# Seven block products for eight in the pooled gate of a two-layer decoder trunk

## The chip, the core and the metric

The kernel runs on one core of a Trainium2 chip. TensorE (PE; its weight loads are listed as PEld) multiplies 128x128 blocks and writes PSUM. VectorE (DVE), ScalarE (ACT) and GpSimd (POOL) work in SBUF. SP issues most of the transfers, and each engine takes its instructions in the order in which they stand in its queue. The metric is the device time of one execution in microseconds, as the median of several runs.

## The reference

Two decoder layers work on 528 tokens (16 learned meta tokens in front of 512), model width 1024, in float32. Each layer makes one projection of the normalised stream, runs two token mixers on its parts, and adds the gated sum of both back:

```
h = rmsnorm(h_res, norm_gain[l])
proj = h @ w_in[l]
u_pool, z_pool, c_q, c_kv, k_rope, z_mla, g_pool, g_mla = jnp.split(proj, IN_SPLIT_POINTS, axis=-1)
y_pool = (pool_mix(u_pool, ...) * jax.nn.silu(z_pool)) @ pool_w_up[l]
o_mla = mla(c_q, c_kv, k_rope, ...)
y_mla = (o_mla * jax.nn.silu(z_mla)) @ mla_w_up[l]
merged = jax.nn.sigmoid(g_pool) * y_pool + jax.nn.sigmoid(g_mla) * y_mla
h_res = h_res + merged @ w_out[l]
```

`pool_mix` takes causal means over windows of 2, 4, 8 and 16 tokens. `mla` is causal attention with 8 heads, a normalisation of queries and keys and a rotary part. The "pooled gate" of the title is `g_pool`, 1024 outputs of the 1024 inputs, thus eight tiles of 128 outputs with eight input blocks of 128 each. The output leaves the meta tokens out. The inputs' gains are scaled by 8, the meta tokens by 3.559.

## The kernel before, in words

**Precision.** Every large product is made from three passes. A float32 operand is split into a rounded high part and a residual: ACT copies the high part in fp32r, DVE subtracts it (`split`, L275, and for weights `wload`, L170 to L182). `mm3` (L184) then multiplies high by high, high weight by low input, and low weight by high input into one PSUM bank.

**The stream of weights.** `register` (L909) appends every matrix product of a layer to `plan` as a `Gemm`, in the order ckv, cq0 to cq4, u with k, v, zp with y, cq5, qr and qn (queries), pu (pooled output), zm, gp (the pooled gate), gm (the other gate), mu and o. `stream` (L193) walks through the plan as a generator in chunks of 512 weight columns, which are four input blocks of a tile. For each chunk it takes the oldest of four prepared ones, issues the load, ACT split and DVE residual of a later chunk, and issues the matmuls. It yields after every second block what these should take, columns over 2.4 GHz, so that the rest of the code can count planned time. Weight chunks arrive in three `raw` buffers on SP's queue; three `whi`/`wlo` pairs hold the split ones.

**Layer input.** x times the norm's gain is split into the eight pairs `hh`/`hl` (`split_h`, L332), without the reciprocal norm of the token. That one, `self.inv` (tile `rinv`), is known later, so it is multiplied in at eviction: L496 for u, L505 for zp and zm, L573 for the pooled gate, L873 for the other one.

**Segments.** Layer 0 computes all 528 tokens, in two halves of 264 columns, each in its own PSUM bank. Layer 1 (`last`) needs only the 512 true tokens for most products, in one segment of 512. Tiles named `mm` share four PSUM banks; the attention's transposes (L796) and its output pieces (L824) take theirs from the same four. Scores have three banks (`S`) and the head's output has one (`o`).

**Attention as host for the gates.** `go` (L973) drives a layer. After the queries come their norm statistics (`qk_stats`, L665) and the preparation of head 0; then eight heads follow. Each head has its scores, a masked row minimum on DVE (L730), exponentials on ACT (L737), row sums, a multiplication on POOL (L774, L776), and transposes and output products one head later (`pv`, L779). Four times per head `gap` (L970) lets the stream run for `FILL[l]` of planned time, so pu, zm, gp and most of gm are worked off between the pieces of the heads. `fill_now` does the same at fixed places. What is issued is then put in order by a scheduler at build time, so the pieces interleave on each engine.

**The gate's eviction.** For each tile m and segment `ev_gp` (L570) multiplies PSUM by `rinv` on DVE (L573), takes tanh on ACT (L574), and DVE forms (tanh + 1) times the pooled output in place (L575; `self.am[m]` is `xb[:, m]`, which held x before). The residual `wlo` of each weight chunk is L181, its high part L180.

Of the kernel before, what the change touches and what calls it, by code (L numbers as in the profile page):

```python
# [9 lines left out]
F32 = mybir.dt.float32  # L10
# [8 lines left out]
P = 128  # L19
# [33 lines left out]
FILL = (2950.0, 2850.0)  # L53
# [18 lines left out]
def trunk(ctx, tc, xT, pos, win, wkr, wqb, wkb, wvb, wgr, wpu, wmu, wout, gains, const, yT):  # L72
# [23 lines left out]
    def sqt():  # L96
        return tp.tile([P, HALF], F32, tag="sq", name=nm("sq"), bufs=14)

# [68 lines left out]

    loads = [0]
# [15 lines left out]
    def mm3(out, wh, wl, xh, xl, start, stop):  # L184
        pe.matmul(out, wh, xh, start=start, stop=False)  # L185
        pe.matmul(out, wh, xl, start=False, stop=False)  # L186
        newest[0] = pe.matmul(out, wl, xh, start=False, stop=stop)  # L187
# [5 lines left out]
    def stream():  # L193
# [3 lines left out]
        def load(i):  # L197
            g_, c = flat[i]
            n = min(512, g_.width - c)
            return wload(g_.src[:, c:c + n], n, g_.gain, g_.spare)  # L200
# [109 lines left out]

    hbuf = [(slot(f"hh{k}", F32R), slot(f"hl{k}", F32R)) for k in range(8)]

    class Layer:
        def __init__(self, l):
            self.l, self.last = l, l == DEPTH - 1
            self.XS = XTOK if self.last else FULL
            self.x0 = NM if self.last else 0
            self.xt = xt if l == 0 else [None] * 8
# [7 lines left out]
            self.sq = []  # L326
            self.st = self.acc = self.inv = self.cinv = self.kraw = self.kp = None
# [171 lines left out]
        def ev_silu(self, dst, tag, m):  # L499
            def ev(ps, a, b):  # L500
                if a == self.x0:
                    dst[m] = slot(f"{tag}{m}") if tag == "u" else xb[:, m]
# [6 lines left out]
            return ev  # L509

# [59 lines left out]
        def ev_gp(self, m):  # L570
            def ev(ps, a, b):
                t = tmp()
                dve.tensor_mul(t[:, :b - a], ps, self.inv[:, a:b])  # L573
                act.activation(t[:, :b - a], t[:, :b - a], AF.Tanh, scale=0.5)  # L574
                dve.scalar_tensor_tensor(out=self.am[m][:, a:b], in0=t[:, :b - a], scalar=1.0,  # L575
                                         in1=self.am[m][:, a:b], op0=ALU.add, op1=ALU.mult)
            return ev
# [87 lines left out]
        def qk_stats(self):  # L665
# [20 lines left out]
            fill_now(9500)  # L686
# [28 lines left out]
        def head(self, h, kq, prev):  # L715
            kh, kl, qh, ql = kq
            odd = h % 2
            nqs = self.nqs
# [6 lines left out]
            def scores(i, out, a, b):  # L725
                q0 = NM + P * i
                mm3(out, qh[:, q0:q0 + P], ql[:, q0:q0 + P], kh[:, a:b], kl[:, a:b], True, True)
# [51 lines left out]
        def pv(self, prev, js):  # L779
# [38 lines left out]
            if odd == 1:  # L818
# [3 lines left out]
                def part2():  # L822
# [5 lines left out]
                    dve.tensor_mul(f, f, self.zms[p][:, NM:T])  # L828
# [34 lines left out]
        def meta_out(self, p):  # L863
            f = tmp()
            dve.tensor_mul(f[:, 0:NM], self.mo[:, NM * p:NM * (p + 1)], self.zms[p][:, 0:NM])
# [43 lines left out]
        def register(self, nxt):  # L909
# [24 lines left out]
            def zp(m):  # L934
                add(f"zp{m}", wi(MT_ZP + m), D, evac=self.ev_silu(self.zps, "xa", m), xs=hs, segs=XS)
# [20 lines left out]
            for m in range(4):  # L956
                add(f"zm{m}", wi(MT_ZM + m), D, evac=self.ev_silu(self.zms, "u", m), xs=hs, segs=XS)
            for m in range(8):
                add(f"gp{m}", wi(MT_GP + m), D, evac=self.ev_gp(m), xs=hs, segs=XS)
# [13 lines left out]
        def go(self, nxt):  # L973
            l = self.l
            up = lambda name: upto((l, name))
            if l == 0:
# [11 lines left out]
            up("u1")  # L988
            for m in range(2):
                self.mix(m, self.window(m))  # L990
            up("u3")
            s2 = self.window(2)
            up("k3")
            s3 = self.window(3)
            up("zp0")
            self.mix(2, s2)
            up("zp1")
            self.mix(3, s3)
            self.k_factors()
            up("qr1")  # L1000
            for s, (a, b) in enumerate(FULL):
                a0 = max(a, self.x0)
                self.stat(self.acc[:, a0:b], a0, b, C_CQ, self.acc_last)
            up("qn3")
            self.qk_stats()
            fill_now(2600)
# [103 lines left out]
```

## Time and profile before

| | |
|---|---|
| time, median of 3 runs | 790.52 us (789.74 to 790.87) |
| span of the profiled execution, first to last instruction | 787.1 us |
| median less span (start and end outside the instructions) | 3.4 us |
| matmuls recorded | 5301 |
| weight chunks split (L180, L181) | 251 and the first |
| transfers | 81.83 MB, mean 104 GB/s |
| first score matmul of head 0, layer 0 and 1 | 174.6 and 571.5 us |
| stage of the pooled gate's evictions, layer 0 and 1 | 210 to 274 and 605 to 658 us |

One execution of its own was profiled; its total is not listed apart from its span. A row of a group names line, engine, operation, tiles and shape, then the count, the total busy time, the mean of one in ns, and the idle time before it with what ended it. Matmul ends are modelled and overlap, so their pace is read from starts. Idle time of an engine that is not the bottleneck costs nothing.

### The profile page before, as it was taken

To read this page: it belongs to the slowest core of one execution; us is meant where nothing else is said; L and a number is where in the kernel's file an instruction comes from. 1 tells how busy PE (TensorE), PEld (TensorE's weight loads), DVE (VectorE), ACT (ScalarE), POOL (GpSimd) and SP (SyncE) were. 2 spreads that over 40 slices of the span, in tenths; PEclk is the share of its full clock that TensorE was granted. 3 is DMA by queue.
4 is the path that set the end of the run, shared out by engine and by line. 5 is a ranking of instruction groups with operands and counts; after the bars stand their busy time and mean duration, and the time that the engine had idled before them with its cause. 6 is when DMAs were issued, how large, how long until landed. Compare 5 with 4: busy or idle time off the path is not lost.

```text
span 787.1 us, 14567 instructions
## 1 busy us (share of the span) xinstructions
PE 780.9 (99%) x5301; PEld 708.6 (90%) x5301; DVE 535.1 (68%) x1165; ACT 410.8 (52%) x930; POOL 194.4 (25%) x259
## 2 busy tenths in 40 slices
PE   9999999999999999999999999999999999999998
PEld 8999899999999999999997898887788888887887
DVE  5848787446779987675464487775467888755932
ACT  7645655635656565633354356455445666554420
POOL 1034504002333242051000145131022333410500
PEclk9999999999999999999999999999999999999999
DMA  6242333423223212224642422334232222122372
GB/s 242 82 102 85 96 120 102 128 81 94 96 76 92 78 58 78 95 81 146 192 123 94 95 88 90 129 88 136 96 105 88 95 84 82 65 81 67 102 242 84
DMA packets 52263, 81.83 MB, mean 104 GB/s; under 512 B 8784, under 2 KB 17360, under 8 KB 52192
## 3 DMA queue, kind: packets, MB, share of 16 engines
q1 hardware_dynamic: 52048, 80.65, 32.9%
q8 instruction: 41, 0.67, 0.4%
q14 instruction: 30, 0.25, 0.1%
q10 hardware_dynamic: 144, 0.26, 0.1%
HBM read 74.49 MB, written 4.27 MB: 100 GB/s over the span
## 4 chain that ended last, share of the span: by engine, by line
PE 95%; DMA 2%; DVE 1%; issue 1%; ACT 0%; SPq 0%; ACTq 0%
PE mm L185 28%; PE mm L187 28%; PE mm L186 28%; PE mm L796 2%; PE S L186 2%; PE S L187 1%; PE S L185 1%; PE o L802 1%; PE o L801 1%; PE S L453 1%; DMA xb<-xT 1%; PE mm L355 1%; DVE wlo L181 1%; PE mm L412 0%; DMA rinv<-win 0%
## 5 line engine op out<-in xcount | busy, mean ns | idle before, releaser
L185 PE MATMUL mm<-hh,whi 128*128 128x264 f32 (+2 forms) x1096 | 346.7, 318 | 0.2 <-ACT racc L810 0.2
L186 PE MATMUL mm<-hl,whi 128*128 128x264 f32 (+2 forms) x1096 | 343.9, 315 | 0.0
L187 PE MATMUL mm<-hh,wlo 128*128 128x264 f32 (+2 forms) x1096 | 343.0, 315 | 0.0
L181 DVE TENSOR_TENSOR wlo<-raw,whi 128x512 fp32r<-128x512 f32 (+2 forms) x251 | 188.6, 755 | 119.6 <-ACT whi L180 115.9
L180 ACT ACTIVATE whi<-raw 128x512 fp32r<-128x512 f32 (+2 forms) x251 | 150.4, 601 | 187.5 <-PE mm L186 126.5
L185 PEld LDWEIGHTS mm<-hh,whi 128*128 128x128 f32 x1096 | 205.9, 188 | 13.6 <-ACT racc L810 0.5
L186 PEld LDWEIGHTS mm<-hl,whi 128*128 128x128 f32 x1096 | 206.6, 189 | 11.8
L187 PEld LDWEIGHTS mm<-hh,wlo 128*128 128x128 f32 x1096 | 205.5, 188 | 12.0
L774 POOL TENSOR_TENSOR pm<-pa,rs 128x16 f32<-128x16 f32 x32 | 11.6, 361 | 181.3 <-DVE rs L769 181.3
L560 POOL TENSOR_TENSOR racc<-racc,tmp 128x264 f32<-128x264 f32 (+1 forms) x15 | 14.2, 948 | 153.8 <-ACT tmp L559 129.8
L702 POOL TENSOR_TENSOR tmp<-kp,bc 64x528 f32<-64x528 f32 x16 | 22.5, 1408 | 76.9 <-PE mm L675 44.5
L884 POOL TENSOR_TENSOR tmp<-tmp,xb 128x264 f32<-128x264 f32 (+1 forms) x24 | 27.1, 1149 | 58.2 <-DVE tmp L882 33.1
L730 DVE CUSTOM_DVE_ANT_0 S<-S,maskw,nqs 128x272 f32<-128x272 f32 (+4 forms) x80 | 38.5, 498 | 4.2 <-PE S L187 3.9
L737 ACT ACTIVATE cq<-S,bia 128x400 f32<-128x400 f32 (+2 forms) x48 | 24.6, 516 | 22.6 <-DVE bia L764 12.0
L185 PE MATMUL mm<-u,whi 128*128 128x264 f32 (+1 forms) x108 | 35.2, 326 | 0.0
L187 PE MATMUL mm<-cq,wlo 128*128 128x264 f32 (+1 forms) x108 | 34.5, 323 | 0.7 <-DVE wlo L181 0.7
L187 PE MATMUL mm<-u,wlo 128*128 128x264 f32 (+1 forms) x108 | 34.8, 323 | 0.0
L185 PE MATMUL mm<-cq,whi 128*128 128x264 f32 (+1 forms) x108 | 34.6, 320 | 0.0
L186 PE MATMUL mm<-cq,whi 128*128 128x264 f32 (+1 forms) x108 | 34.5, 321 | 0.0
L277 DVE TENSOR_TENSOR tl<-mm,th 128x512 fp32r<-128x512 f32 (+1 forms) x64 | 29.3, 481 | 6.1 <-ACT th L276 5.1
L776 POOL TENSOR_TENSOR cq<-cq,rs 128x384 f32<-128x384 f32 (+1 forms) x32 | 32.8, 1025 | 0.0
L186 PE MATMUL mm<-kn,whi 128*128 128x264 f32 (+1 forms) x96 | 30.7, 321 | 0.0
(252 smaller groups left out, 1362.4 us busy)
## 6 DMA issues: line engine op xcount, KB each, us to landing
raw<-win SPq DMA_DIRECT2D x143, 256.0 KB, 2.6
raw<-wout SPq DMA_DIRECT2D x32, 256.0 KB, 2.7
bc<-kdr SPq DMA_DIRECT2D x16, 264.0 KB, 3.6
raw<-wpu SPq DMA_DIRECT2D x16, 256.0 KB, 2.7
raw<-wmu SPq DMA_DIRECT2D x16, 256.0 KB, 2.5
raw<-wqb SPq DMA_DIRECT2D x12, 256.0 KB, 2.6
tmp<-xT SPq DMA_DIRECT2D x16, 132.0 KB, 3.0
tmp<-scr SPq DMA_DIRECT2D x7, 256.0 KB, 3.4
```

Of the source, the lines that this page charges most:

```text
L180: act.activation(hi[:, :n], raw[:, :n], AF.Copy)
L181: dve.tensor_sub(lo[:, :n], raw[:, :n], hi[:, :n].bitcast(F32))
L185: pe.matmul(out, wh, xh, start=start, stop=False)
L186: pe.matmul(out, wh, xl, start=False, stop=False)
L187: newest[0] = pe.matmul(out, wl, xh, start=False, stop=stop)
L277: dve.tensor_sub(lo[:, a:b], src, hi[:, a:b].bitcast(F32))
L702: gp.tensor_mul(kf[r0:r0 + 64, :], self.kp[r0:r0 + 64, :], bc[r0:r0 + 64, :])
L730: dve.tensor_tensor_reduce(out=sv, in0=sv, in1=mask, scale=nqs[:, i, h:h + 1], scalar=3e38, op0=ALU.add, op1=ALU.min, accum_out=bia[:, c:c ...
L737: act.activation(pv, sv, AF.Exp, scale=-1.0, bias=bia[:, i:i + 1], accum_out=rs[:, c:c + 1])
L776: gp.tensor_mul(pt[i][:, NM:], pt[i][:, NM:], rs[:, i:i + 1].to_broadcast([P, n - NM]))
L796: pe.transpose(tr[:, P * (i - j):P * (i - j + 1)], pt[i][:, NM + P * j:NM + P * (j + 1)], ident)
L884: gp.tensor_add(t[:, :b - a], t[:, :b - a], self.am[m][:, a:b])
```

## The change

The eight gate tiles are taken in four pairs and the input in two halves of four blocks and two halves of tokens. Each pair is then a 2x2 product of blocks, and Strassen's scheme in Winograd's form makes it from seven products in place of eight. That takes sums of weight blocks and of input blocks, and additions of the products.

- *Input sums.* They need one input for both token halves, so the input must be fully normalised. `reload` fetches blocks 0 to 3 of x anew from DRAM (blocks 4 to 7 still lie in `xb`), `renorm` multiplies each of the eight by gain and `rinv` and writes `hh`/`hl` again, and `mixed` forms the four sums per block pair and splits them. This stands behind the first query tiles, in and behind the query statistics, and in head 0.
- *Weight sums.* `weight_sums` forms them in DRAM (`wsum`), from copies issued by SP and accumulating transfers issued by POOL, in ten steps from the second u tile to the third query tile. Each waits for the newest matmul.
- *Products.* `fast` registers one Gemm with 28 chunks. Product 2 accumulates on product 1's bank, and product 3 of one pair on product 5's bank, after the next pair's product 1. ACT copies product 1; the others are combined by five DVE additions or subtractions per pair.
- *Evictions.* As the input is normalised, `got_gp`, `ev_zm` and `ev_gm` leave the multiplication by `rinv` out. A factor of a half of the silu of z_mla moves into the multiplications by `zms`.
- *Constants.* `FILL` shrinks, some fixed fills around the query statistics change, and in head 0 a score product is held behind the newest matmul.

```diff
-FILL = (2950.0, 2850.0)
+FILL = (2770.0, 2700.0)
...
-    def mm3(out, wh, wl, xh, xl, start, stop):
-        pe.matmul(out, wh, xh, start=start, stop=False)
...
+    def mm3(out, wh, wl, xh, xl, start, stop, more=False, hold=False):
+        first = pe.matmul(out, wh, xh, start=start, stop=False, skip_group_check=more)
+        if hold:
+            behind(first, newest[0])
...
+        def ev_zm(self, m):
+            def ev(ps, a, b):
...
+                act.activation(t[:, :b - a], ps, AF.Tanh, scale=0.5)
+                dve.scalar_tensor_tensor(out=self.zms[m][:, a:b], in0=t[:, :b - a], scalar=1.0, in1=ps,
+                                         op0=ALU.add, op1=ALU.mult)
...
+        def reload(self, k):
+            self.f[k] = slot("kl" if k % 2 else "kh", bufs=2)
+            sp.dma_start(self.f[k][:, self.x0:T], scr[:, k, :] if self.last else xT[:, k, :])
+
+        def renorm(self, k):
...
+            f, (hh, hl) = self.f[k][:, self.x0:T], self.hs[k]
+            dve.scalar_tensor_tensor(out=f, in0=x[:, self.x0:T], scalar=self.g(G_H + k), in1=self.inv[:, self.x0:T],
+                                     op0=ALU.mult, op1=ALU.mult)
+            split(hh, hl, f, self.x0, T)
+
+        def mixed(self, k):
...
+            dve.tensor_sub(w[:, b:c], u[:, b:c], w[:, b:c])
+            dve.tensor_sub(u[:, b:c], u[:, a:b], u[:, b:c])
+            dve.tensor_sub(u[:, a:b], u[:, a:b], w[:, b:c])
+            dve.tensor_sub(w[:, a:b], w[:, a:b], u[:, a:b])
+            split(th, tl, u[:, a:c], a, c)
+            for h_, l_, v in ((t3h, t3l, w[:, b:c]), (t4h, t4l, w[:, a:b])):
+                split(h_, l_, v, 0, n)
...
+        def fast(self, name, w, got):
+            order = []
+            for u in range(4):
+                order += [(1, u)] + [(3, u - 1)] * (u > 0) + [(p, u) for p in (6, 7, 2, 5, 4)]
+            order.append((3, 3))
...
+                for k in range(4):
+                    xh, xl = (t[:, s[0]:s[1]] for t in self.hs[k + o]) if p < 4 else self.tt[k][p]
+                    c = P * k
+                    mm3(ps, w_[0][:, c:c + P], w_[1][:, c:c + P], xh, xl, k == 0 and p not in (2, 3), k == 3, True)
...
+                if p == 1:
+                    v["q", u] = q = svt()[:, :n]
+                    act.activation(q, ps, AF.Copy)
+                elif p == 2:
+                    got(2 * u, A, ps, True)
+                elif p == 6:
+                    v["u", u] = t = svt()[:, :n]
+                    dve.tensor_sub(t, v["q", u], ps)
+                elif p == 7:
+                    v["v", u] = t = svt()[:, :n]
+                    dve.tensor_sub(t, ps, v["u", u])
+                elif p == 5:
+                    t = tmp()[:, :n]
+                    dve.tensor_sub(t, v["v", u], ps)
+                    got(2 * u + 1, B, t, False)
...
+        def weight_sums(self, i, w):
...
+                if s == 0:
+                    for i, t in enumerate((b[:, 0:512], a[:, 0:512], a[:, 0:512], a[:, 512:1024])):
+                        behind(sp.dma_start(d[:, i, :], t), newest[0])
+                else:
+                    for i, t in ((0, b[:, 512:1024]), (2, b[:, 0:512])):
+                        behind(gp.dma_start(d[:, i, :], t, accum_op=ALU.add), newest[0])
+            if 0 < u < 5:
+                d = wsum[l][u - 1]
+                behind(gp.dma_start(d[:, 3 if s else 1, :], d[:, 1 if s else 0, :], accum_op=ALU.add), newest[0])
...
-                t = tmp()
-                dve.tensor_mul(t[:, :b - a], ps, self.inv[:, a:b])
-                act.activation(t[:, :b - a], t[:, :b - a], AF.Tanh, scale=0.5)
-                dve.scalar_tensor_tensor(out=self.am[m][:, a:b], in0=t[:, :b - a], scalar=1.0,
-                                         in1=self.am[m][:, a:b], op0=ALU.add, op1=ALU.mult)
...
+        def got_gp(self, m, s, v, psum):
+            am = self.am[m][:, s[0]:s[1]]
+            t = tmp()[:, :s[1] - s[0]] if psum else v
+            act.activation(t, v, AF.Tanh, scale=0.5)
+            dve.scalar_tensor_tensor(out=am, in0=t, scalar=1.0, in1=am, op0=ALU.add, op1=ALU.mult)
...
-            fill_now(9500)
+            for k in range(2):
+                self.mixed(k)
+                fill_now(2000)
+            for k in range(2, 4):
+                self.renorm(k)
+                self.renorm(k + 4)
+                fill_now(2500)
...
-                d = self.gms[m][:, a:b]
-                dve.tensor_mul(d, ps, self.inv[:, a:b])
-                act.activation(d, d, AF.Tanh, scale=0.5)
+                act.activation(self.gms[m][:, a:b], ps, AF.Tanh, scale=0.5)
...
-            for m in range(8):
-                add(f"gp{m}", wi(MT_GP + m), D, evac=self.ev_gp(m), xs=hs, segs=XS)
+            self.fast("gp", [wi(MT_GP + m) for m in range(8)], self.got_gp)
...
+            up("qn0")
+            sums()
+            for k in range(2):
+                self.renorm(k)
+                self.renorm(k + 4)
+                up(f"qn{k + 1}")
+            sums()
             up("qn3")
             self.qk_stats()
-            fill_now(2600)
             kq = self.prep(0)
             fill_now(2600)
+            self.mixed(2)
...
             for h in range(H):
                 kn_ = self.head(h, kq, prev)
                 self.gap()
+                if h == 0:
+                    self.mixed(3)
```

More of the change, by code (lines that the diff above doesn't have):

```diff
@@ L717, in head @@
             odd = h % 2
-            nqs = self.nqs
+            nqs, hold = self.nqs, h == 0
             pa = slot("pa", bufs=2, w=416)
@@ L726, in scores @@
                 q0 = NM + P * i
-                mm3(out, qh[:, q0:q0 + P], ql[:, q0:q0 + P], kh[:, a:b], kl[:, a:b], True, True)
+                mm3(out, qh[:, q0:q0 + P], ql[:, q0:q0 + P], kh[:, a:b], kl[:, a:b], True, True,
+                    hold=hold and i == 1)
             def top(i, c, sv, mask):
@@ L975, in go @@
             up = lambda name: upto((l, name))
+            made = iter(range(10))
+            sums = lambda: self.weight_sums(next(made), [win[l, MT_GP + m] for m in range(8)])
             if l == 0:
@@ L999, in go @@
             self.k_factors()
+            sums()
+            up("zp3")
+            sums()
+            up("cq5")
+            sums()
+            up("qr0")
+            sums()
+            for k in range(4):
+                self.reload(k)
             up("qr1")
```

91 lines of the change are left out of this document (79 added, 12 removed).

## The prediction

> **What bounds the kernel now.** I read the page first, its busy line, its slices and its chain of waits.
>
> ```profile
> span 787.1 us, 14567 instructions
> PE 780.9 (99%) x5301; PEld 708.6 (90%) x5301; DVE 535.1 (68%) x1165; ACT 410.8 (52%) x930; POOL 194.4 (25%) x259
> PE   9999999999999999999999999999999999999998
> DVE  5848787446779987675464487775467888755932
> PEclk9999999999999999999999999999999999999999
> PE 95%; DMA 2%; DVE 1%; issue 1%; ACT 0%; SPq 0%; ACTq 0%
> ```
>
> TensorE is busy in every slice at the full granted clock, and 95% of the chain runs through it, so a matmul less is time less as long as no other engine takes over. The slices say where that could happen: VectorE stands at 9 in slices 13, 14 and near it in 29 to 33. These are the two attention stages, where the gate's tiles are used as filling between the heads. The windows of those stretches, read next, give length, PE, PEld, DVE, ACT and POOL busy time, clock and DMA share. The gate's own evictions (L573 to L575) fill 210 to 274 in layer 0 and 605 to 658 in layer 1.
>
> ```profile
> 210.00:274.00 64.00, 64.00 (x523) 63.19 (x523) 56.47 (x136) 39.53 (x101) 19.56 (x28) 1.00 0.26 84
> 605.00:658.00 53.00, 53.00 (x280) 45.10 (x279) 45.50 (x101) 33.16 (x81) 19.19 (x29) 1.00 0.28 85
> ```
>
> In the gate's stage VectorE is busy 56.5 of 64.0 us and 45.5 of 53.0: TensorE still sets the pace, with only 7.5 us to spare on VectorE in each.
>
> **The change, part by part: TensorE.** A matmul's recorded time overlaps the next one's, so its price is the distance of starts, read from the timeline in three stretches without a gap (start, duration):
>
> ```profile
> 299.76 0.29 PE L185 MATMUL mm<-hh,whi 128*128 128x264 f32 x1
> 301.10 0.29 PE L187 MATMUL mm<-hh,wlo 128*128 128x264 f32 x1
> ...
> 752.99 0.39 PE L185 MATMUL mm<-hh,whi 128*128 128x512 f32 x1
> 756.92 0.40 PE L187 MATMUL mm<-hh,wlo 128*128 128x512 f32 x1
> ...
> 778.78 0.28 PE L186 MATMUL mm<-hl,whi 128*128 128x256 f32 x1
> 783.51 0.28 PE L187 MATMUL mm<-hh,wlo 128*128 128x256 f32 x1
> ```
>
> The pairs are 11, 17 and 40 starts apart: 0.122 us for 264 columns, 0.231 for 512, 0.118 for 256. Layer 0 had 8 tiles x 8 blocks x 3 x 2 halves = 384 matmuls of 264 (46.8 us) and gets 4 pairs x 7 products x 4 blocks x 3 = 336 (41.0): -5.8 us. Layer 1 had 192 of 512 (44.4) and gets 336 of 256 (39.7): -4.7 us. Together **-10.5 us**, all on the path. The Trainium skill (TensorE: Matmul & The Clock Gate, "Wait — 56ns, not 53.3ns?") puts a warm matmul at its columns over 2.4 GHz plus about 2.5 ns, so 112, 216 and 109 ns; by that rule the saving is 10.1 us, and since the trace's starts are wider, the trace decides.
>
> **VectorE in the gate's stage.** Durations by line and form:
>
> ```profile
> L181 DVE TENSOR_TENSOR wlo<-raw,whi 128x512 fp32r<-128x512 f32 x223 | 175.0, 787 | 111.5 <-ACT whi L180 110.0
> L573 DVE TENSOR_TENSOR tmp<-mm,rinv 128x264 f32<-128x264 f32 x16 | 6.7, 424 | 0.3
> L573 DVE TENSOR_TENSOR tmp<-mm,rinv 128x512 f32<-128x512 f32 x8 | 5.5, 689 | 4.2 <-PE mm L187 4.2
> L575 DVE SCALAR_TENSOR_TENSOR xb<-tmp,xb 128x512 f32<-128x512 f32 x8 | 5.5, 684 | 0.5 <-ACT tmp L574 0.4
> ```
>
> and the timeline, for what a full queue pays:
>
> ```profile
> 247.78 0.42 DVE L575 SCALAR_TENSOR_TENSOR xb<-tmp,xb 128x264 f32<-128x264 f32 x1
> 248.12 0.41 DVE L573 TENSOR_TENSOR tmp<-mm,rinv 128x264 f32<-128x264 f32 x1
> 248.46 0.62 DVE L730 CUSTOM_DVE_ANT_0 S<-S,maskw,nqs 128x400 f32<-128x400 f32 x1
> ...
> 250.99 0.68 DVE L181 TENSOR_TENSOR wlo<-raw,whi 128x512 fp32r<-128x512 f32 x1
> 251.59 0.55 DVE L277 TENSOR_TENSOR tl<-mm,th 128x384 fp32r<-128x384 f32 x1
> ...
> 262.99 1.28 DVE L181 TENSOR_TENSOR wlo<-raw,whi 128x512 fp32r<-128x512 f32 x1
> ...
> 262.69 1.04 POOL L776 TENSOR_TENSOR cq<-cq,rs 128x512 f32<-128x512 f32 x1
> ```
>
> Back to back, the next instruction starts 0.08 us before the end of the one before: 0.34 us for 264 columns, 0.61 for 512. The residual at 262.99 took 1.28 us beside a POOL operation that ended at 263.73, and 0.68 alone; over all 223 the mean is 787 ns, 0.10 above that. So a residual costs 0.71.
>
> A product needs a full 512-column weight chunk for only half the columns of x. The gate's chunks go from 16 to 28 per layer, and each is one ACT split and one VectorE residual: +12 x 0.71 = 8.5 us. The products' recombination is 5 additions per pair, 20 per layer. Layer 0 loses 16 multiplications by the norm (L573) of the same width: +4 x 0.34 = 1.4. Layer 1 loses 8 of 512 (4.9) for 20 of 256 (6.7), and its 8 closing operations (4.8) become 16 (5.4): +2.4. In the built order the heads that carry the gate hold 6 to 8 weight residuals each, where they held 3 to 6. The fills shrink as well. In planned time (columns over 2.4 GHz) layer 0's gate was 42.2 us over fills of 2.95, 14.3 of them; now it is 37.0 over 2.77, 13.3. In layer 1 it was 41.0 over 2.85, 14.4, and is 35.8 over 2.70, 13.3. So one fill's worth of attention, a quarter head, leaves the stage. Per fill that is what remains after the gate's own work: (64.0 - 46.8) / 14.3 = 1.2 us of PE and (56.5 - 11.4 - 5.4 - 5.4) / 14.3 = 2.4 of VectorE in layer 0; in layer 1, (53.0 - 44.4) / 14.4 = 0.6 and (45.5 - 11.4 - 4.9 - 4.8) / 14.4 = 1.7, times 1.1 fills 0.7 and 1.9.
>
> Layer 0 then wants 56.5 + 8.5 + 1.4 - 2.4 = 64.0 us of VectorE against 64.0 - 5.8 - 1.2 = 57.0 of TensorE. Layer 1 wants 45.5 + 8.5 + 2.4 - 1.9 = 54.5 against 53.0 - 4.7 - 0.7 = 47.6. **VectorE becomes the longer queue in both stages**, by 7 us. Some of the busy time is the 0.08 us tails that vanish in a full queue (some 35 gaps, 3 us), so the excess is 4 to 7. TensorE starts the stage with up to two split chunks in hand (three buffers, 1.5 us each), which hides up to 3; a queue in strict order also waits for ACT, and the busiest head window shows what is attainable (length, VectorE busy):
>
> ```profile
> 262.30:278.70 16.40, 16.03 (x38) 1.00 0.25 84
> ```
>
> 98%, so 1 to 3 us of 60 are lost again. I take **5.5 us of TensorE idle per layer, 11 in both**, bounds 0 (all hidden) and 9 per layer (excess 7 without cover, 2 lost). ACT goes from 39.5 of 64 by 12 splits and 4 copies, under 10 us, and stays below TensorE.
>
> **The second input and the query stage.** Each layer gains 4 reloads of x, 8 normalisations with splits and 4 mixings of two blocks. Rows for the operations, and the windows where they will stand (columns as above):
>
> ```profile
> L338 DVE SCALAR_TENSOR_TENSOR hl<-xb,gn,hh 128x528 fp32r<-128x528 f32 x15 | 10.9, 764 | 4.0 <-ACT hh L336 4.0
> L277 DVE TENSOR_TENSOR kl<-tmp,kh 128x528 fp32r<-128x528 f32 x16 | 11.6, 726 | 4.9 <-ACT kh L276 4.8
> 135.00:155.00 20.00, 20.00 (x179) 18.73 (x177) 10.45 (x16) 12.60 (x31) 3.59 (x4) 1.00 0.42 115
> 155.00:175.00 20.00, 20.00 (x164) 19.66 (x163) 9.14 (x25) 9.49 (x22) 1.33 (x1) 1.00 0.28 91
> 520.00:535.00 15.00, 14.35 (x62) 11.34 (x62) 12.47 (x17) 9.89 (x23) 8.37 (x6) 1.00 0.28 80
> ```
>
> Eight times 0.76 + 0.73 is 11.9 us; a mixing is six 264-column operations and a split, 6 x 0.34 + 0.65 = 2.7, three of them 8.1 before head 0. That is 20 us of VectorE into 40 with 19.6 busy: it just fits, behind weights of 2.6 us a chunk split up to three ahead, and I cost it at 0, at 4 if the cover is gone. The stretch 520 to 535 already has 0.65 us of TensorE idle: the rotary steps go DVE, POOL, ACT, DVE, and the weight residual stands behind the last. There the change puts normalisations into the same queue and accumulating transfers into POOL's, which wait for the newest matmul with the rotary steps behind them: +1.5 us, bounds 0 and 6.
>
> ```profile
> q1 hardware_dynamic: 52048, 80.65, 32.9%
> raw<-win SPq DMA_DIRECT2D x143, 256.0 KB, 2.6
> ndr<-ny SPq DMA_DIRECT2D x4, 2.0 KB, 8.9
> ACT whi L180 <- PE mm L186: 126.5, 90, 3.4
> ACT whi L180 <- DMA raw<-win: 5.1, 4, 3.4
> ```
>
> Transfers: 80.65 MB took 32.9% of 787 us, so 256 KB is 0.84 us of the sixteen engines; 16 copies, 16 accumulations (two reads and a write, estimated double), 4 reloads and 12 more weight chunks are about 54 us per layer in some 90 us that are two thirds free, and the splits have waited for PE's buffers (126.5 us) far more than for weights (5.1). No row shows an accumulating transfer: between 2.6 us (a load) and 8.9 (the slowest small write); nearest is the load. The Trainium skill (DMA: Bandwidth & Descriptors, "Anatomy of one DMA — SWDGE (gpsimd) path") gives 2.0 us plus the bytes at 436 GB/s, 2.6 us here; by it the sum stays the same, and no run so far shows it. The sums are wanted 50 us later. SP's copies wait for the newest matmul with raw loads behind them, but the next raw load waits for a buffer that falls free later than that: 0. The shorter gm and zm evictions lie where TensorE bounds: 0. The matmul order forced in head 0 is PE's own: 0.
>
> **Sum.** -10.5 + 11 + 1.5 = +2.0 us. The profiled span goes from 787.1 to 789.1; the runs' median lies 3.4 us above the span, so **792.5 us**. Under 0.2% (1.6 us) this measurement tells nothing from no change.
>
> **The rivals.** *Fully hidden*: the buffers and the lighter stages around the gate take the excess, TensorE idles 0 to 5 us. For it speaks that 98% busy cost TensorE nothing at 262 to 279; against it, that such a head would have to last for four heads running. -10.5 + 3 gives 783. *Banks (slower)*: a pair holds a PSUM bank from product 1 to product 2 and another from product 5 to the next pair's product 3, so of four banks two are left for products 6, 7, 4, the head's transposes and the output pieces. A bank is reused only after its VectorE operation, which now stands in a full queue. If 8 reuses per pair come 1 us late, that adds up to 8 us per layer to a queue that is late itself; with half of it overlapping, 792.5 + 8 = 801. It decides as soon as VectorE runs more than one product behind. *POOL held up*: if accumulations take 8.9 us and hold POOL, the rotary step, and behind it every residual, is late by 4 to 6 us in both layers: 801 as well, and it would show at 120 to 160 and 515 to 550, not in the heads.
>
> **How the numbers follow.** Forecast (VectorE bounds the gate, 788 to 798): 0.5; hidden: 0.3; banks: 0.15; POOL: 0.05. The range 782 to 803 leaves out the lowest hidden and the deepest bank cases; the forecast's own is 788 to 798. Faster by over 0.2%: the hidden case and 0.04 of the forecast's, 0.34. Same: 0.11. Slower: 0.55.
>
> **What would show it.** Matmul starts 0.122 and 0.118 apart in the gate; in the heads that hold it DVE at 95% or more with TensorE gaps released by DVE's wlo and evictions, 4 to 7 us in each layer. Wrong, if TensorE stays without gaps there (783), if the gaps come from ACT or DMA, or if idle time sits in the query stage.

## The result, and the profile after

The changed kernel takes 834.14 us (833.08 to 836.06, 4 runs) against 790.69 (789.74 to 791.9, 4 runs) in the same session: ratio 1.055, 95% interval 1.053 to 1.057. It is slower by 43 us, and far above the range of 782 to 803.

From the page of the profile after: span, busy time, slices, chain of waits.

```profile
span 833.4 us, 15164 instructions
PE 791.4 (95%) x5397; PEld 715.9 (86%) x5397; DVE 579.5 (70%) x1265; ACT 441.8 (53%) x1010; POOL 228.5 (27%) x291
PE   9999887999999899999999998988999999999998
PEclk9999898999999999999999999899999999999999
DMA  6246588652345332234642557887433453223272
PE 72%; DMA 13%; DVE 8%; issue 3%; ACT 2%; POOL 1%; SPq 0%; ACTq 0%; DVEq 0%; POOLq 0%
```

TensorE's part of the chain fell from 95% to 72%, and DMA rose from 2% to 13%. The slices (20.8 us each) say where: from the fifth to the seventh (83 to 146 us) and the 25th to the 28th (500 to 583) TensorE drops to 7 and 8 in six of seven, the transfers stand at 5 to 8, and the granted clock falls to 8 in three of them. These are the keys, values and queries of each layer, before any gate tile; the 14th slice, also at 8 for TensorE, belongs to the gate's heads. The windows of those two stretches and of the two in which the gate fills the heads (length, PE, PEld, DVE, ACT, POOL busy, clock, DMA share, GB/s), after:

```profile
60.00:205.00 145.00, 129.47 (x997) 121.57 (x996) 103.10 (x238) 78.45 (x182) 45.65 (x52) 0.94 0.63 150
240.00:300.00 60.00, 54.84 (x425) 51.80 (x423) 58.45 (x133) 40.75 (x104) 27.11 (x36) 1.00 0.45 126
480.00:600.00 120.00, 108.57 (x572) 85.15 (x572) 89.69 (x179) 63.64 (x139) 44.73 (x48) 0.96 0.71 168
655.00:705.00 50.00, 45.22 (x348) 42.82 (x347) 47.25 (x107) 33.37 (x83) 21.66 (x27) 1.00 0.45 128
```

and the first and third of them before:

```profile
60.00:205.00 145.00, 145.00 (x1193) 139.50 (x1193) 101.02 (x243) 81.61 (x197) 38.12 (x48) 1.00 0.33 99
480.00:600.00 120.00, 119.35 (x566) 95.33 (x566) 78.99 (x160) 62.14 (x130) 23.14 (x27) 1.00 0.33 104
```

The gate's own stages came out as forecast: VectorE busy 58.45 of 60 and 47.25 of 50, TensorE idle 5.2 and 4.8 us. The 43 us are elsewhere. TensorE idles 15.5 and 11.4 us in the two earlier stretches, and what it does there runs at a clock of 0.94 and 0.96, while the DMA share doubles. The chain in 90 to 145 us (start, us, what) says what ended the idle time:

```profile
90.49 7.48 DMA kh<-xT
97.99 0.52 DVE kh L544
...
107.39 7.06 DMA raw<-wgr
114.54 0.32 ACT whi L186
...
116.18 7.89 DMA raw<-win
124.15 0.64 ACT whi L186
...
133.44 9.56 DMA raw<-wqb
143.11 0.63 ACT whi L186
```

Three of the four transfers are weight loads that take 7 to 10 us to land, with the split and then TensorE behind them. The first is the reload of x. Its reader (L544, the first operation of `renorm`) stands among the evictions of the values in VectorE's queue, so the values wait for a transfer that they don't need. The DMA issues (count, KB each, median us to landing) after; before, raw<-wqb landed in 2.6 and 2.1 us, raw<-wvb in 2.6, raw<-wgr in 2.3:

```profile
wsum<-win SPq DMA_DIRECT2D x32, 256.0 KB, 6.8
wsum<-win POOLq DMA_DIRECT2D x16, 256.0 KB, 7.5
wsum<-wsum POOLq DMA_DIRECT2D x16, 256.0 KB, 7.8
raw<-wqb SPq DMA_DIRECT2D x12, 256.0 KB, 4.8
raw<-wvb SPq DMA_DIRECT2D x4, 256.0 KB, 4.6
raw<-wgr SPq DMA_DIRECT2D x8, 64.0 KB, 6.2
```

A ledger from the starts of matmuls after the first 20 us: every distance that is over 0.25 us longer than the pace (0.122 us for 264 columns, 0.231 for 512, 0.118 for 256, others in proportion), less the pace, summed. It gives 45.0 us after and 2.2 before. Of the 45.0, 18.1 lie in 60 to 205, 14.4 in 480 to 600, 6.5 and 6.0 in the two stretches of gate heads. The lost clock (one less the granted clock, times the length) is 13.7 us after the first 20 us; 3.4 us of the stretches at half clock are idle time that the ledger has already, so some 12 us come on top. -10.5 for the matmuls saved, +42.8 and +12.0 make +44.3; the span of the profiled execution grew by 46.3.

### The profile page after: what moved, and what is told of

It reads as the page before. It is cut to its first block, busy times and chain, and to the rows that moved or that the text cites. A ratio compares the mean times of both kernels' runs of the same rounds, so it can differ in the third digit from the quotient of the medians.

```text
span 833.4 us, 15164 instructions
## 1 busy us (share of the span) xinstructions
PE 791.4 (95%) x5397; PEld 715.9 (86%) x5397; DVE 579.5 (70%) x1265; ACT 441.8 (53%) x1010; POOL 228.5 (27%) x291
## 4 chain that ended last, share of the span: by engine, by line
PE 72%; DMA 13%; DVE 8%; issue 3%; ACT 2%; POOL 1%; SPq 0%; ACTq 0%; DVEq 0%; POOLq 0%
PE mm L191 21%; PE mm L195 21%; PE mm L194 21%; DMA raw<-win 3%; DMA raw<-wqb 3%; DVE wlo L187 2%; DMA raw<-wvb 2%; DMA raw<-wgr 2%; PE mm L931 1%; ACT whi L186 1%; PE S L194 1%; PE S L195 1%; PE S L191 1%; PE o L937 1%; DMA kh<-xT 1%
## 5 line engine op out<-in xcount | busy, mean ns | idle before, releaser
L191 PE MATMUL mm<-hh,whi 128*128 128x264 f32 (+2 forms) x1000 | 314.1, 316 | 10.8 <-ACT whi L186 6.7
L195 PE MATMUL mm<-hh,wlo 128*128 128x264 f32 (+2 forms) x1000 | 311.1, 314 | 2.3 <-DVE wlo L187 2.3
L194 PE MATMUL mm<-hl,whi 128*128 128x264 f32 (+2 forms) x1000 | 310.9, 312 | 0.0
L191 PEld LDWEIGHTS mm<-hh,whi 128*128 128x128 f32 x1000 | 189.6, 190 | 25.2 <-ACT whi L186 12.6
L194 PEld LDWEIGHTS mm<-hl,whi 128*128 128x128 f32 x1000 | 190.0, 190 | 9.6
L191 PE MATMUL mm<-cq,whi 128*128 128x264 f32 (+2 forms) x172 | 55.4, 323 | 8.2 <-ACT tmp L690 5.8
L195 PE MATMUL mm<-cq,wlo 128*128 128x264 f32 (+2 forms) x172 | 54.5, 321 | 1.9 <-DVE wlo L187 1.9
L909 POOL TENSOR_TENSOR pm<-pa,rs 128x16 f32<-128x16 f32 x32 | 11.3, 353 | 159.6 <-DVE rs L904 141.1
L194 PE MATMUL mm<-cq,whi 128*128 128x264 f32 (+2 forms) x172 | 54.3, 316 | 0.0
L691 POOL TENSOR_TENSOR racc<-racc,tmp 128x264 f32<-128x264 f32 (+1 forms) x15 | 14.8, 987 | 115.0 <-ACT tmp L690 115.0
L191 PEld LDWEIGHTS mm<-cq,whi 128*128 128x128 f32 x172 | 33.9, 197 | 11.4 <-ACT tmp L690 6.0
L865 DVE CUSTOM_DVE_ANT_0 S<-S,maskw,nqs 128x400 f32<-128x400 f32 (+4 forms) x80 | 38.5, 499 | 3.4 <-PE S L195 2.9
L195 PEld LDWEIGHTS mm<-cq,wlo 128*128 128x128 f32 x172 | 33.8, 197 | 4.8 <-DVE wlo L187 2.9
L194 PEld LDWEIGHTS mm<-cq,whi 128*128 128x128 f32 x172 | 34.0, 198 | 1.6
L285 DVE TENSOR_TENSOR tl<-mm,th 128x512 fp32r<-128x512 f32 (+1 forms) x64 | 29.5, 483 | 8.1 <-ACT th L284 7.6
```

Source lines behind the costliest of these rows:

```text
L191: first = pe.matmul(out, wh, xh, start=start, stop=False, skip_group_check=more)
L194: pe.matmul(out, wh, xl, start=False, stop=False, skip_group_check=more)
L195: newest[0] = pe.matmul(out, wl, xh, start=False, stop=stop, skip_group_check=more)
L285: dve.tensor_sub(lo[:, a:b], src, hi[:, a:b].bitcast(F32))
L691: self.acc_last = gp.tensor_add(self.acc[:, a:b], self.acc[:, a:b], t[:, :b - a])
L865: dve.tensor_tensor_reduce(out=sv, in0=sv, in1=mask, scale=nqs[:, i, h:h + 1], scalar=3e38, op0=ALU.add, op1=ALU.min, accum_out=bia[:, c:c ...
```

## The experiments

Theories at the start. **A**: the weight sums' transfers make the weight loads late, by the accumulations (**A1**) or by the copies in SP's queue (**A2**). **B**: the second input is normalised too early in VectorE's queue. **C**: the gate's stage, as forecast.

| run | us (range) | ratio to before, 95% |
|---|---|---|
| changed kernel | 834.1 (833.1 to 836.1) | 1.055 (1.053 to 1.057) |
| e1 no sums' transfers | 804.7 (803.6 to 806.2) | 1.020 (1.018 to 1.021) |
| e2 copies only | 811.2 (810.4 to 815.3) | 1.029 (1.026 to 1.031) |
| e3 normalisation pinned | 829.7 (828.6 to 832.1) | 1.051 (1.049 to 1.053) |
| e4 normalised input, eight products | 796.3 (794.1 to 796.9) | 1.008 (1.007 to 1.010) |
| e5 plain transfers for the adding ones | 818.0 (817.6 to 821.4) | 1.036 (1.033 to 1.038) |
| e6 = e1, no gate residuals | 792.5 (791.1 to 794.4) | 1.003 (1.002 to 1.004) |
| e7 = e1, pinned | 796.0 (795.3 to 796.9) | 1.007 (1.005 to 1.009) |
| e8 layer 1's sums early | 826.6 (825.7 to 829.4) | 1.046 (1.044 to 1.049) |
| e9 = e4, pinned | 792.0 (791.0 to 793.3) | 1.003 (1.002 to 1.004) |
| e10 = e6, pinned | 786.5 (786.4 to 786.8) | 0.996 (0.995 to 0.998) |
| e11 = e8, pinned | 819.3 (818.1 to 823.9) | 1.039 (1.036 to 1.041) |
| e12 = e11, layer 0's sums one by one | 808.1 (807.0 to 809.1) | 1.022 (1.020 to 1.024) |

**Taking the parts away: e1 to e4.** e1 makes no sums, and loads plain blocks of win where sums were loaded (the second edit, on `src` in `fast`, is left out here):

```diff
-            sums = lambda: self.weight_sums(next(made), [win[l, MT_GP + m] for m in range(8)])
+            sums = lambda: None
```

> Leaves out the weight sums altogether (no copies, no accumulating transfers); products 5, 6, 7 and 3 load plain weight blocks of the same size instead, so the gate's values are not the reference's while every matmul, split and addition stays. Theory A (the sums' transfers make the weight loads of the projection and query stages late): nearly all TensorE idle time between 60 and 205 us and between 480 and 600 us goes (15.6 and 11.5 us of idle, and most of the 13 us that the lower granted clock costs there), so 834 falls to about 796 to 803, and weight loads land in 2.6 us again. Theory B (the renormalisation and its reloads stand in VectorE's queue too early and block it): the sums matter little, 834 falls by 10 at most, to 824. Theory C (the gate's stage among the heads is what costs): no change in the first stages, under 5 us.

e2 leaves the accumulations out and keeps the copies:

```diff
-                else:
-                    for i, t in ((0, b[:, 512:1024]), (2, b[:, 0:512])):
-                        behind(gp.dma_start(d[:, i, :], t, accum_op=ALU.add), newest[0])
-            if 0 < u < 5:
-                d = wsum[l][u - 1]
-                behind(gp.dma_start(d[:, 3 if s else 1, :], d[:, 1 if s else 0, :], accum_op=ALU.add), newest[0])
```

> Leaves out the sixteen accumulating transfers of each layer that POOL issues and keeps the sixteen copies that SP issues, so the gate's weights are not sums and its values are not the reference's. Theory A1 (accumulating transfers are the expensive part, with 7.5 to 7.8 us each and 7.6% of the DMA engines' span): 834 falls most of the way to e1_no_sums, to about 805 to 812. Theory A2 (copies in SP's own queue ahead of the weight loads are the expensive part, 6.8 us each): it stays above 820. If both only matter together (bandwidth), it lands between.

e3 ties the first operation of `renorm` to the newest matmul:

```diff
-            dve.scalar_tensor_tensor(out=f, in0=x[:, self.x0:T], scalar=self.g(G_H + k), in1=self.inv[:, self.x0:T],
-                                     op0=ALU.mult, op1=ALU.mult)
+            behind(dve.scalar_tensor_tensor(out=f, in0=x[:, self.x0:T], scalar=self.g(G_H + k),
+                                            in1=self.inv[:, self.x0:T], op0=ALU.mult, op1=ALU.mult), newest[0])
```

> All work kept; each of the eight renormalisations per layer waits for the newest matmul at the place where the code calls it, so the scheduler can no longer put it ahead in VectorE's queue (built order: behind the query tiles instead of among the values' evictions). Theory B: the waits of DVE for the reload (6.1 us in the trace, longest 5.6) and the TensorE gaps at 96 to 101 and 515 to 520 us (4.5 and 4.1 us, and the lower clock behind them) go: 834 falls by 8 to 14, to 820 to 826. Theory A: the loads are late all the same and the gap moves to the next late load: 834 falls by under 5.

e4 keeps the normalised input and goes back to eight products, without sums and mixing, with `FILL` of before (the changed fixed fills stay):

```diff
-            self.fast("gp", [wi(MT_GP + m) for m in range(8)], self.got_gp)
+            for m in range(8):
+                add(f"gp{m}", wi(MT_GP + m), D, evac=self.ev_g8(m), xs=hs, segs=XS)
```

> The normalised input alone: reloads, renormalisation and the evictions without the norm stay; the gate is made from eight products again, with no weight sums, no input sums and the fills of before. The output is the reference's. Theory A or C: little is left that costs, 790 to 795 (the gate's and the other gate's evictions are lighter than before, the renormalisation costs up to 5 us where it stands early). Theory B: the block in VectorE's queue is still there, 798 to 806.

Sessions differ by about 1 us (the kernel before took 789.4 to 790.7), so a difference between runs of two of them is no finer than that. The transfers are the largest part: 834.1 - 804.7 = 29.5 us, of which the 16 copies per layer are 6.6 (811.2 - 804.7) and the accumulations the rest. e2 still has 32 copies in SP's queue, so A2 isn't the main part. Pinning is worth 4.4 us beside the sums. The normalised input with eight products (e4) costs 6.9 us over before, and the seven products without sums (e1) a further 8.4: even with no transfer for sums the change does not pay.

**What the adding costs: e5.** The same sixteen transfers per layer, in the same queue behind the same matmuls, with `accum_op=ALU.add` taken out, so that they write copies in place of sums:

```diff
-                        behind(gp.dma_start(d[:, i, :], t, accum_op=ALU.add), newest[0])
+                        behind(gp.dma_start(d[:, i, :], t), newest[0])
```

> The changed kernel took 834.1 us, with the sixteen accumulating transfers per layer left out 811.2, and with all of the sums' transfers left out 804.7. Here the sixteen transfers stay where they are, in POOL's queue and behind the same matmuls, but write a plain copy instead of adding, so the summed weights are not the sums. If it is the adding itself that costs (a second read and a slower landing), sixteen more copies cost about what the first sixteen did, 6.6 us: 816 to 820, with the weight loads landing near 4 us. If it is only their number and bytes, or that POOL's queue issues them, whatever they do: 830 to 835, and the loads land as late as in the changed kernel (raw<-wqb 4.8, raw<-wgr 6.2 us).

818.0: the adding itself is 16.1 us, and sixteen more plain transfers are 6.8, as much as the first sixteen. The DMA issues of e5:

```profile
raw<-wqb SPq DMA_DIRECT2D x12, 256.0 KB, 4.9
wsum<-win POOLq DMA_DIRECT2D x16, 256.0 KB, 4.1
wsum<-wsum POOLq DMA_DIRECT2D x16, 256.0 KB, 5.2
```

The transfers that no longer add land in 4.1 and 5.2 us in place of 7.5 and 7.8. One expectation missed: raw<-wqb is as late as ever (4.9), so its median does not follow the time. The other late loads do follow it: raw<-wvb falls from 4.6 to 2.9 us and raw<-wgr from 6.2 to 4.3.

**The gate's stage: e6.** On top of e1, the gate's chunks get no residual (the rounded half stands in for it), so TensorE's matmuls stay and 56 VectorE operations go:

```diff
+        if whole:
+            return hi, hi
         dve.tensor_sub(lo[:, :n], raw[:, :n], hi[:, :n].bitcast(F32))
```

> The kernel without the sums' transfers (804.7 us), with the seven-product tiles' weight residuals left out as well: 56 VectorE operations of about 0.7 us less, all in the gate's stages; the products use the rounded half in the residual's place, so TensorE does the same matmuls. If VectorE is what holds TensorE up in those heads (gaps of 4.3 us in layer 0 and 5.9 in layer 1, and a clock that falls nowhere there), the gaps go: 794 to 796. If the gaps come from the banks that a pair of tiles holds, or from the loads, they stay: 803 to 805.

The windows of the gate heads, e1 and then e6:

```profile
220.00:282.00 62.00, 56.76 (x438) 53.65 (x438) 59.23 (x137) 42.28 (x110) 27.14 (x37) 1.00 0.39 122
625.00:675.00 50.00, 45.18 (x355) 43.33 (x355) 47.24 (x108) 33.29 (x85) 21.65 (x27) 1.00 0.40 128
```

```profile
220.00:282.00 62.00, 60.23 (x487) 58.98 (x486) 50.14 (x123) 44.63 (x115) 24.74 (x37) 1.00 0.46 135
620.00:670.00 50.00, 48.68 (x363) 46.01 (x363) 40.79 (x97) 35.69 (x93) 19.02 (x28) 1.00 0.41 125
```

792.5, 12.1 us less. With VectorE at 50 of 62 and 41 of 50, TensorE's idle time falls from 5.2 and 4.8 us to 1.8 and 1.3. So 7.0 of the 10.1 us of idle time were VectorE's load. The rest of the 12.1 us lies mostly outside the gate's heads: in e1 the clock stands at one half for 3.4 us at 128 and again at 568, in e6 at neither place. That makes 3.4 us of lost clock, and neither place is in the gate's stage. e6 by itself does not settle the banks, since a lighter VectorE also frees them sooner; the waits of TensorE do. What is left in e6 is in the main two waits for the addition of product 4, which frees a bank (1.4 and 1.1 us).

**The place of the normalisation: e7, e9.** e7 is e1 and e9 is e4, each with the edit of e3.

> The kernel without the sums' transfers (804.7 us), with the first operation of each normalisation kept behind the newest matmul, so that it cannot move up among the values' evictions. If the early place costs by itself, the gaps of 1.35 us near 67 and 1.26 near 470 go and those at 104 to 125 and 525 to 565 shrink: 800 to 802. If it only mattered because the reloads landed late beside the sums (it was worth 4.4 us there): 804 to 806, or more, since the splits then stand in the query stage's queue.

> The kernel with the normalised second input alone (eight products, no sums, no mixing; 796.3 us), with the first operation of each normalisation kept behind the newest matmul. If the early place of the normalisation is all that the second input costs, the gaps of 1.35, 1.0, 2.1, 1.3, 1.1 and 1.1 us go and the granted clock with them, some 8 us: 787 to 790, at or just under the kernel before (790.6), because 16 and 8 VectorE multiplications by the norm have left the gate's stages. If the second input costs VectorE time wherever it stands: 794 to 797.

e7 takes 796.0, 8.7 us less than e1, and more than expected. What the early place does is seen in e1's timeline (start, us):

```profile
65.84 2.34 DVE L544 SCALAR_TENSOR_TENSOR xb<-xb,gn,rinv 128x528 f32<-128x528 f32 x2 [0.66 <-PE mm L425]
68.11 0.42 DVE L712 TENSOR_TENSOR kn<-mm,q 128x264 f32<-128x264 f32 x1
```

Blocks 4 and 5 are normalised at 65.8 us, as soon as L425 has read them and far ahead of their place in the code, and a key's eviction (L712) stands behind them. TensorE needs that bank, and its starts are 1.35 us late. In e7 the gaps there and at 124 us are gone: TensorE is busy 144.3 of the 145 us from 60 to 205, where e1 had 141.1. The pin is worth twice as much here as in e3; I take it that there the late loads held TensorE up with or without it.

e9 takes 792.0 and not 787 to 790: the second input alone, in its place, still costs 2.4 us over the 789.5 of its session. Its window of the query stage, layer 1:

```profile
530.00:542.00 12.00, 10.10 (x37) 7.64 (x36) 11.93 (x15) 8.49 (x18) 5.20 (x4) 0.86 0.25 66
```

VectorE is full there (11.93 of 12), TensorE loses 1.9 us, and the clock falls behind it. The gate heads are lighter on VectorE (45.5 us of 240 to 300, where before had 52.3), but TensorE had no idle time there to win.

**Both cures together: e10.**

> Seven products without the sums' transfers, with both cures together: the normalisation kept behind the newest matmul (alone 796.0 us) and the seven-product tiles' weight residuals left out (alone 792.5), against 804.7 with neither. If the two losses are separate, their savings of 8.7 and 12.1 us add up: 783 to 785, so that of the forecast's 10.5 us of fewer matmuls at least 6 are there when VectorE is not in the way. If they are the same idle time seen twice: 789 to 793.

786.5, ratio 0.996: the savings add up to 18.2 of the 20.8 expected, so they are mostly separate. This is the fully hidden rival, with VectorE's load taken out by force: 3.0 us under before, of 10.5 saved. Of the remaining 7.5, 4.9 are late starts (the ledger's 7.1 us against 2.2 before) and 1.7 lost clock at 535 to 538, behind the query stage of layer 1; some 0.9 stay unexplained.

**Where and how the sums are made: e8, e11, e12.** e8 makes layer 1's sums in layer 0's last heads:

```diff
                 self.pv(prev, (2, 3))
+                if h >= 4:
+                    sums1()
                 prev = kn_
                 self.gap()
+                if h >= 3:
+                    sums1()
+            sums1()
```

> The changed kernel (834.1 us), with layer 1's sums made during layer 0's last five heads instead of during layer 1's first stages; nothing else is changed. If the sums cost because of the stage in which they stand (values, keys, queries, with small dependent loads and two late engines), layer 1's share, about 13 us of TensorE gaps and lost clock, goes: 818 to 824. If they cost by their bytes wherever they stand, the gaps move to layer 0's end at 300 to 420 us: 830 to 836.

826.6, 7.6 us less. The place matters and not only the bytes: in e8's windows TensorE loses 1.5 us where most of the sums now stand, at a DMA share of 0.62, and in 480 to 600 it is where e1 has it (115.4). The first batches stand ahead of the first window, at 283 to 300 us, and are not free: TensorE is busy 17.7 of the 20 us from 280 at a clock of 0.91, in the changed kernel 18.3 at 1.00.

```profile
300.00:440.00 140.00, 138.53 (x1122) 136.85 (x1123) 84.52 (x180) 66.24 (x151) 34.53 (x46) 1.00 0.62 153
480.00:600.00 120.00, 115.38 (x643) 94.76 (x642) 101.75 (x202) 68.89 (x148) 35.94 (x33) 0.99 0.37 108
```

The gain is little more than half of what I had put to layer 1's share, and why the later heads bear such transfers so well was not separated. e11 adds the pin of e3:

> The whole change with its sums (834.1 us), with layer 1's sums made during layer 0's last heads (alone 826.6) and the normalisation kept behind the newest matmul (alone 829.7; without any sums worth 8.7). If both savings hold, layer 1's first stages lose neither to the sums nor to the early normalisation: 816 to 823. If layer 0's late loads hide what the pin gains: 822 to 827.

819.3, 14.8 us less than the changed kernel: the two savings (7.6 and 4.4) add up, and a little more. In e12 layer 0's 32 transfers stay in their queues and start at the same place in the code. The last three adding ones fall behind the stretch, at 213 to 228 us, since all are issued one by one in place of batches:

```diff
-            sums()
+            if l == 0:
+                self.sums_apart([win[l, MT_GP + m] for m in range(8)])
...
+            for j, fn in enumerate(jobs):
+                after(4000.0 * j, fn)
```

> The whole change with layer 1's sums early and the normalisation kept in place (819.3 us), and layer 0's 32 transfers issued one by one, 4 us of planned matmul time apart, in place of ten batches of 4 to 8. If the sums cost because a batch fills the sixteen DMA engines for some microseconds (their share stands at 1.0 just before the gaps) while weight loads wait among it, the loads land near 3 us again and the gaps near 121 and 138 go: 803 to 810. If it is their bytes and their adding, however they are spread: 816 to 822.

808.1, 11.3 us less with the same transfers. (The batches were of one to five, not four to eight: four copies and one adding transfer, then three adding ones.) The window of 60 to 205 us, e11 and then e12:

```profile
60.00:205.00 145.00, 134.82 (x1035) 127.20 (x1034) 107.10 (x250) 80.78 (x193) 51.24 (x53) 0.94 0.64 153
```

```profile
60.00:205.00 145.00, 140.37 (x1144) 133.83 (x1143) 116.43 (x275) 87.15 (x205) 47.61 (x57) 1.00 0.64 155
```

The mean DMA share is 0.64 in both, yet TensorE has 5.5 us more and its clock is whole. In windows of 1 us, 48 of e11's 145 stand at a share of 0.9 or more, with up to nine in a row; in e12 they are 28, at most four in a row (before: 3, none in a row). e5, which also lost less, has 26, at most four in a row. e12 takes the copies out of SP's queue in fours as well, and how much of the 11.3 that is was not separated; all the copies in fours, of both layers, cost 6.6 in e2. This is the best form of the whole change that was found, and it is 2.2% slower than before.

## Why the prediction was wrong

**TensorE, -10.5: right.** From after's timeline of the gate (start, duration), each pair eight starts apart:

```profile
246.77 0.29 PE L191 MATMUL mm<-hh,whi 128*128 128x264 f32 x1
247.74 0.28 PE L195 MATMUL mm<-hh,wlo 128*128 128x264 f32 x1
...
678.71 0.28 PE L191 MATMUL mm<-hh,whi 128*128 128x256 f32 x1
679.66 0.28 PE L195 MATMUL mm<-hh,wlo 128*128 128x256 f32 x1
```

0.97 / 8 = 0.121 and 0.95 / 8 = 0.119, as forecast.

**VectorE in the gate's stage, +11: right in place and size, and in the main in cause.** 5.2 and 4.8 us of idle TensorE were measured against 5.5 forecast, VectorE stood at 97% and 94.5%, and without its residuals (e6) 7.0 of e1's 10.1 us go. The releasers are more mixed than forecast. TensorE's longest waits after, in 240 to 300 and then in 655 to 705 (us, times, longest):

```profile
PE mm L931 <- POOL cq L911: 1.3, 1, 1.3
PE mm L191 <- DVE tmp L610: 1.1, 1, 1.1
PE o L937 <- DVE tl L285: 0.8, 2, 0.7
PE mm L195 <- DVE wlo L187: 0.6, 1, 0.6
...
PE o L937 <- DVE tl L285: 2.5, 2, 1.6
PE mm L195 <- DVE wlo L187: 1.4, 3, 0.9
```

VectorE ended 6.9 of the 9.9 us, but its wlo only 2.0; 3.3 are the head's own residual (L285), which stands in the same full queue. POOL and ACT ended 3.0. The saving on TensorE was paid back for the most part on VectorE, as the sum said.

**"Transfers: ... 0": the step that failed**, with 29.5 us. The amount was about right. By the windows of 60 to 205 the DMA share is 0.33 without sums (e1), 0.42 with the copies (e2) and 0.63 with all: 0.09 x 145 / 16 = 0.82 us of all engines for a copy (0.84 forecast), and 0.21 x 145 / 16 = 1.9 for an adding transfer (1.7). What failed was to set that sum against an average share of a third. The transfers go out in batches: four copies and one adding transfer are 4 x 0.82 + 1.9 = 5.2 us of all sixteen engines, the next three adding ones 5.7, and where two batches run together the engines are full for up to nine windows of 1 us in a row (50 of 145 stand at 0.9 or more, 3 before). A load issued into that lands 7 to 10 us later, and the cover that the prediction counted, two or three split chunks of 1.5 us, doesn't reach so far. e12 supports it: the same bytes spread out cost 11.3 us less. The price of an adding transfer, 2.6 to 8.9 with 2.6 taken as nearest, was near the other end: 7.5 and 7.8 us. The Trainium skill (DMA: Bandwidth & Descriptors, "Anatomy of one DMA — SWDGE (gpsimd) path") gave the same 2.6 us as an estimate; the trace does not agree for these transfers, which add from DRAM to DRAM among others: even as plain copies they took 4.1 and 5.2 (e5).

**The second input, 0 (4 if the cover is gone): too small, 8.7 us without the sums (e7), 4.4 beside them (e3).** The prediction took its place from the code, behind the first query tiles, and read the windows from 135 and from 520 us for it. In the order that was built, VectorE's first operations of it stand among the keys' and values' evictions, where one waits for the reload (6.1 us in two waits; the longest, 5.6, at 92 to 98 us) and the others hold a bank up. Put back into the place that the prediction assumed (e9), it costs 2.4 us.

**The query stage, +1.5 (0 to 6): about right for what it spoke of.** e9, which has the normalisations without the sums, loses 1.9 us there. The rival at 801, *POOL held up*, had the price of an adding transfer nearly right (7.5 and 7.8 us against its 8.9), and TensorE is idle where it would show, but not by its mechanism: between 115 and 165 and between 510 and 590 us no piece of the chain lies on POOL and no engine waits for it; the chain there runs over late loads.

**The clock: no step at all.** The sum had no term for it. Some 12 us of the loss are TensorE running at half speed behind its gaps.

**Small readings.** The VectorE slices called "near" 9 are 32 to 34, and not 29 to 33 (29 stands at 4); the windows, from which the sum goes, are read rightly. The 3.4 us between span and time compare a median with another execution: nearly all runs here take 1.7 to 2.1 us longer than their own span. Neither changes the outcome.

**The rivals.** Fully hidden did not occur, and e10 shows what it needed. Banks: waits for an operation that frees a bank (the products' subtraction at L610, the output pieces' addition at L962) ended 1.6 us in layer 0's gate heads and none in layer 1's, against 8 per layer in the rival. The forecast named "idle time sits in the query stage" as what would refute it; it sat there, and in the stages ahead of it.

## What to carry to other kernels

A mean DMA share doesn't say what a batch of transfers does: take the time for which the batch fills all engines, and compare it with how far ahead the loads behind it were issued. An operation whose inputs are early will be scheduled early; its place has to be read from the built order, or tied. A product saved on the engine that bounds is worth only what the engine that prepares its operands has to spare, and here the preparing (12 chunks more per layer) and the additions took back nearly all that the products saved.

## What the runs showed of the hardware

A gap on TensorE of some 2 us or more can cost twice. In the changed kernel the gaps of 3.0 us at 96, 3.2 at 121, 5.9 at 138, 2.3 at 516 and 2.2 at 562 each bring 3.4 or 6.8 us at a granted clock of 0.50. This starts between 1.2 us ahead of the gap's end and 1.7 us behind it. Single gaps of 1.8 us and less do not. The windows around the first, second, third and fourth (clock ahead of the DMA share):

```profile
98.00:106.00 8.00, 5.97 (x25) 5.15 (x26) 7.39 (x15) 1.29 (x3) 0.00 (x0) 0.57 0.39 114
120.00:130.00 10.00, 6.94 (x43) 6.69 (x43) 4.84 (x12) 3.05 (x7) 0.00 (x0) 0.83 0.71 213
137.00:150.00 13.00, 7.24 (x39) 7.03 (x38) 8.27 (x20) 4.66 (x12) 2.61 (x3) 0.74 0.81 204
516.00:526.00 10.00, 7.17 (x19) 5.02 (x18) 7.71 (x17) 2.42 (x7) 0.25 (x1) 0.66 0.38 116
```

Between some 1.8 and 3 us it goes both ways. 2.07 us at 535 in e9 was followed by a fall to 0.50, 2.05 at the same place in e7 was not. By the idle time that the profile lists, 1.86 us at 125 in e1 was followed by a fall, and 2.65 at 571 in e2 and 2.86 at 522 in e3 were not. In e12 the clock falls at 287 to 290 behind three gaps of 0.8, 1.1 and 0.4 us in a row. So no threshold comes out of these runs. The Trainium skill (TensorE: Matmul & The Clock Gate, "Part 1: The HAM clock gate (the "warmup" mystery)") has the clock halved after an idle window of about 3.4 us. The factor of a half agrees with the trace, and a gap of 2.2 us was enough here (at 562).

Adding in a transfer was dearer than its bytes. POOL's transfers for the sums have a DMA queue of their own (packets, MB, share of sixteen engines' span), after and then in e5:

```profile
q0 software_dynamic: 4608, 8.39, 7.6%
q0 software_dynamic: 2560, 8.39, 4.2%
```

For 32 transfers in spans of 833.4 and 819.6 us that is 1.98 us of the sixteen engines for an adding one against 1.08 for the same one without the adding, and the median to landing, from win, was 7.5 us against 4.1.
